# Rows of 520 columns for the normalised and the inner feed-forward activations of a two-layer encoder

## The chip, the cores and the metric

One Trainium2 chip, one core of it. The metric is the device time of one execution in microseconds. The kernel before takes 1377.04 us (median of 3 runs, 1375.52 to 1378.2).

## The reference

A two-layer encoder trunk on 512 tokens of width 1024. Layer 0 mixes by neighbourhood attention and a bidirectional state-space scan, layer 1 by grouped-query attention with rotary positions; each layer ends with a gated feed-forward part. All parts are residual. Cut to what matters here:

```python
def swiglu_ffn(x, norm_g, w13, w2):
    g, u = jnp.split(rms_norm(x, norm_g) @ w13, 2, axis=-1)   # 1024 -> 2 x 2816
    return (jax.nn.silu(g) * u) @ w2                          # 2816 -> 1024

def reference(x, ...):
    for layer in range(2):
        x = x + even_mixer(x, ...) if layer == 0 else x + odd_mixer(x, ...)
        x = x + swiglu_ffn(x, ffn_norm[layer], ffn_w13[layer], ffn_w2[layer])
    return x
```

Everything is float32.

## The kernel before, in words

All 512 tokens are held at once, features across the 128 partitions, tokens along the row: the residual stream is 8 tiles of 128 x 512. Weights are streamed from memory in blocks of 128 x 1024.

Precision comes from splitting each float32 operand into a high part that the matmul's float32r type holds, and the low rest. For the weights `load_w` (L130 to L137) does this: a DMA brings the raw block, the scalar engine writes the high part (L135), the vector engine (or GpSimd) the low one (L136). For the normalised activations `prep` (L160 to L164) does it, into two tiles made by `xgslot` (L93, L94), named xh and xl. `mm3` (L139 to L144) multiplies a split pair in three matmuls of 512 columns that accumulate in one bank: low weights by high activations (L142), high weights by low activations (L143), high by high (L144). The weight block of 128 x 128 is what a matmul loads first; the activation tile is what it streams.

`ffn` (L708 to L743) runs twice. It first splits the 8 residual tiles into 16 tiles xh and xl. Then 22 steps follow, each with one projection for the gate (banks fg) and one for the up half (banks fu), 8 triples of matmuls each; the results are scaled, gated and split again into tiles hh and hl, made by `hlane`, 44 in all. Last come 8 sums (banks fo) of 22 triples each over hh and hl, added to the residual. That is 2 x 22 x 24 = 1,056 matmuls a layer for gate and up and 8 x 66 = 528 for the second products; both layers, 2,112 and 1,056. The mixers' projections (banks g, qps, kps, q and others) stream xh and xl tiles from `xgslot` too. `oA`, layer 0's output projection, streams tiles of the mixer's pool for its first ten blocks; the last two blocks are streamed from `xgslot` tiles by `tail` (banks t), which runs right behind it. The odd layer does the same with banks o and t.

Instructions stand in the order in which this code writes them; each engine waits by semaphores for what it reads. Tiles come from pools, which are laid one behind the other along each partition, so where a tile starts follows from the sizes of the rows before it. In the built program:

| pool | what | first byte in a partition | row of one tile |
|---|---|---|---|
| `xpool`, `sp` | residual, scratch | 20,960 and 37,344 | 2,048 bytes |
| `xgpool` | 16 slots for xh, xl | 61,920 | 2,048 bytes |
| `wsp` | weight blocks, raw, high, low | 94,688 | 4,096 bytes |
| `sm` | small tiles | 127,456 | mixed, 4,320 bytes with the gap |
| `lp`, `hp0`, `op`, `hp1` in turn | mixers' tiles; hh, hl | 131,776 | 2,048 bytes for hh, hl |

From `xgpool` to `wsp` there are 32,768 bytes, a multiple of 512; a weight block of 128 columns is 512 bytes. From `wsp` to the last pools there are 37,088 bytes, 224 more than a multiple of 512.

Of the kernel before, what the change touches and what calls it, by code (L numbers as in the profile page):

```python
# [10 lines left out]
F32R = mybir.dt.float32r  # L11
# [5 lines left out]

P = 128
S = 512
D = 1024  # L20
KB = D // P
EPS = 1e-6
GRID_W = 64
ROWS = S // GRID_W
NA_H = 8
# [39 lines left out]
def encoder_kernel(ctx: ExitStack, tc: tile.TileContext, xt, vec, cst, rope, nab, w_v, w_qk, w_dt, w_ssd,  # L65
# [7 lines left out]
    xgpool = ctx.enter_context(tc.tile_pool(name="xgpool", bufs=2 * KB))  # L73
# [7 lines left out]
    def bank(name, tag="p"):  # L81
        if tag in turns:
            turns[tag].append(turns[tag].pop(0))
            tag = turns[tag][-1]
        return pp.tile([P, S], F32, name=name, tag=f"p{tag}", bufs=BANKS[tag])

    def slot(name, dt=F32):
        return sp.tile([P, S], dt, name=name, tag="s")

    def xslot(name, dt=F32):  # L90
        return xpool.tile([P, S], dt, name=name, tag="x")

    def xgslot(name):  # L93
        return xgpool.tile([P, S], F32R, name=name, tag="xg")  # L94

    def laner(pool):
        def lane(name, tag, bufs, dt=F32, cols=S):
            return pool.tile([P, cols], dt, name=name, tag=tag, bufs=bufs)
        return lane

    def small(name, cols, bufs=3, parts=P, dt=F32):
        return sm.tile([parts, cols], dt, name=name, tag=f"sm_{name}", bufs=bufs)

    def f(ap):
        return ap.bitcast(F32)
# [17 lines left out]
    def sum_rows(ps, sq, name, eng=V):  # L123
        hi, lo = slot(f"{name}_qh", F32R), slot(f"{name}_ql", F32R)
        A.activation(hi, sq, AF.Copy)
        eng.tensor_tensor(lo, sq, f(hi), ALU.subtract)
        T.matmul(ps, ones_r, lo, start=True, stop=False)
        T.matmul(ps, ones_r, hi, start=False, stop=True)

    def load_w(src, cols, name, eng=None):  # L130
        hi = wsp.tile([P, 1024], F32R, name=f"{name}_h", tag="wh", bufs=WH)
        lo = wsp.tile([P, 1024], F32R, name=f"{name}_l", tag="wl", bufs=WL)
        raw = wsp.tile([P, 1024], F32, name=f"{name}_r", tag="wr", bufs=WR)[:, 0:cols]
        nc.sync.dma_start(raw, src)
        A.activation(hi[:, 0:cols], raw, AF.Copy)  # L135
        (eng or V).tensor_tensor(lo[:, 0:cols], raw, f(hi)[:, 0:cols], ALU.subtract)  # L136
        return hi, lo  # L137

    def mm3(ps, w, wc, x, xc, first, last, wn=P):  # L139
        (wh, wl), (xh, xl) = w, x  # L140
        a, b = slice(wc, wc + wn), xc
        T.matmul(ps, wl[:, a], xh[:, b], start=first, stop=False)  # L142
        T.matmul(ps, wh[:, a], xl[:, b], start=False, stop=False)  # L143
        T.matmul(ps, wh[:, a], xh[:, b], start=False, stop=last)  # L144
# [10 lines left out]
    def project(ps, src, xg, name, eng=None):  # L155
        w = load_w(src, 1024, name, eng)
        for k in range(KB):
            mm3(ps, w, k * P, xg[k], ALL, k == 0, k == KB - 1)

    def prep(xt, g, name, mk=xgslot):  # L160
        hi, lo = mk(f"{name}_xh"), mk(f"{name}_xl")
        A.activation(hi, xt, AF.Copy, scale=g)
        V.scalar_tensor_tensor(lo, xt, g, f(hi), ALU.mult, ALU.subtract)  # L163
        return hi, lo  # L164
# [11 lines left out]
    def rsqrt_wide(ps, inv, name):  # L176
        m = slot(f"{name}_m")
        A.activation(m, ps, AF.Identity, scale=inv, bias=epst)
        return rsqrt_tile(m, name)
# [12 lines left out]
    def rsqrt_small(m, r, t):  # L192
        A.activation(r, m, AF.Ln)
        A.activation(r, r, AF.Exp, scale=-0.5)
        V.tensor_tensor(t, r, r, ALU.mult)
        V.tensor_tensor(t, t, m, ALU.mult)
        V.tensor_scalar(t, t, -0.5, 1.5, ALU.mult, ALU.add)
        V.tensor_tensor(r, r, t, ALU.mult)

    def bcast_rstd(acc, name):  # L200
        ps = bank(f"{name}_ss", "c")
        sum_rows(ps, acc, name)
        return rsqrt_wide(ps, 1.0 / D, name)

    res = [None] * KB

    def even_mixer(lp):
# [56 lines left out]
        rt, rtm, rtt = small("rt", 8, 1), small("rtm", 4, 1), small("rtt", 4, 1)  # L264
        V.tensor_scalar(rtm, pst[:, 0:4], 1.0 / D, EPS, ALU.mult, ALU.add)
        rsqrt_small(rtm, rt[:, 0:4], rtt)
# [256 lines left out]
        def ssd_group(g, gt):  # L523
# [114 lines left out]
            for i in range(2):  # L638
                yn = slot(f"yn{g}_{i}")
                V.tensor_tensor(cols(yn), pi(ys[i]), pi(r), ALU.mult)  # L640
                ssd_out[2 * g + i] = prep(yn, vc("out_norm", 2 * g + i), f"so{g}_{i}",
                                          mixslot if g < 3 else xgslot)
# [56 lines left out]
    def prep_all(gname, name):  # L699
        return [prep(res[k], vc(gname, k), f"{name}{k}") for k in range(KB)]  # L700

    def sumsq(name):
        acc = None
        for k in range(KB):
            acc = accsq(acc, res[k], name, G)
        return acc

    def ffn(layer, gname, hp):  # L708
        hlane = laner(hp)
        turns["f"] = ["p", "s", "t", "x", "s", "t", "p"]  # L710

        def fbank(name):
            return bank(name, "f")

        xg = prep_all(gname, f"f{layer}")
        hb = []
        rstd = None
        for i in range(HB):
            gp, up = fbank(f"fg{layer}_{i}"), fbank(f"fu{layer}_{i}")
            project(gp, w_fa[layer, 2 * i], xg, f"wfg{layer}_{i}")  # L720
            project(up, w_fa[layer, 2 * i + 1], xg, f"wfu{layer}_{i}")
            if i == 0:
                rstd = bcast_rstd(sumsq(f"f{layer}"), f"fr{layer}")
            g, s = slot(f"g{layer}_{i}"), slot(f"s{layer}_{i}")
            V.tensor_tensor(g, gp, rstd, ALU.mult)  # L725
            A.activation(s, g, AF.Silu)
            V.tensor_tensor(g, up, rstd, ALU.mult)  # L727
            V.tensor_tensor(g, g, s, ALU.mult)
            hi, lo = hlane(f"hh{layer}_{i}", "h", 2 * HB, F32R), hlane(f"hl{layer}_{i}", "h", 2 * HB, F32R)
            A.activation(hi, g, AF.Copy)  # L730
            V.tensor_tensor(lo, g, f(hi), ALU.subtract)
            hb.append((hi, lo))
        for o in range(KB):
            ps = fbank(f"fo{layer}_{o}")
            k0 = 0
            for j, n in enumerate(W2_SPLIT):
                w = load_w(w_fb[layer, o, :, k0 * P:(k0 + n) * P], n * P, f"wf2{layer}_{o}_{j}")
                for k in range(n):
                    mm3(ps, w, k * P, hb[k0 + k], ALL, k0 + k == 0, k0 + k == HB - 1)
                k0 += n  # L740
            V.tensor_tensor(res[o], res[o], ps, ALU.add)
            if layer == 1:
                nc.sync.dma_start(out[o], res[o])  # L743

    def odd_mixer(op):
# [51 lines left out]
        rt, rtm, rtt = small("ort", 4, 1), small("ortm", 4, 1), small("ortt", 4, 1)  # L797
        V.tensor_scalar(rtm, pst[:, 0:4], 1.0 / D, EPS, ALU.mult, ALU.add)
        rsqrt_small(rtm, rt, rtt)
        ss = bank("oss", "c")  # L800
        T.matmul(ss, ones, acc, start=True, stop=True)
        em = slot("oem")
        V.tensor_scalar(em, ss, EPS / D, EPS * EPS, ALU.mult, ALU.add)

# [206 lines left out]
    with tc.tile_pool(name="hp0", bufs=1, reuse_waits="tile") as hp:  # L1011
        ffn(0, "g_ffn0", hp)
    with tc.tile_pool(name="op", bufs=1, reuse_waits="tile") as op:
        odd_mixer(op)
    with tc.tile_pool(name="hp1", bufs=1, reuse_waits="tile") as hp:
        ffn(1, "g_ffn1", hp)
# [6 lines left out]
def _tiles(w, cols=P):  # L1023
    k, n = w.shape
    return np.ascontiguousarray(w.reshape(k // P, P, n // cols, cols).transpose(2, 1, 0, 3)).reshape(
        n // cols, P, (k // P) * cols)
# [34 lines left out]
def _layout(x):  # L1061
# [41 lines left out]
    a["w_qk"] = _tiles(w[:, 0:1024])  # L1103
    wdt = np.concatenate([w[:, 4608:4640], np.zeros((D, 32), np.float32)], 1)
    a["w_dt"] = np.ascontiguousarray(wdt.reshape(KB, P, 64).transpose(1, 0, 2)).reshape(P, KB * 64)
# [42 lines left out]
```

## Time and profile before

| | |
|---|---|
| runs | 1375.52, 1377.04, 1378.2 us |
| span of the profiled execution | 1375.2 us, first to last instruction; its own time isn't listed apart |
| matmuls (PE) | busy 1326.8 us, 96% of the span |
| weight loads (PEld) | busy 1083.7 us, 79% |
| vector engine (DVE) | busy 820.0 us, 60% |
| scalar engine (ACT) | busy 601.4 us, 44% |
| GpSimd (POOL) | busy 274.6 us, 20% |
| mean granted clock of the matmul engine | 0.988 |

The profile's rows of matmul groups read: line, engine, operation, result<-operands by the program's names, shapes, count, busy time in us, mean duration of one in ns, and the idle time of the engine just before them. A row of the timeline reads: start in us, duration in us, engine, line, operation, result<-operands, shapes, count. A matmul's duration runs past the start of the next, as they are pipelined; the distance between starts is what each one costs. The feed-forward layers stand, in us from the span's start, at about 409 to 797 (layer 0; the odd layer's first projections begin within its last 12 us) and 995 to 1371 (layer 1).

### The profile page before, as it was taken

To read this page: it belongs to the slowest core of one execution; us is meant where nothing else is said; L and a number is where in the kernel's file an instruction comes from. 1 tells how busy PE (TensorE), PEld (TensorE's weight loads), DVE (VectorE), ACT (ScalarE), POOL (GpSimd) and SP (SyncE) were. 2 spreads that over 40 slices of the span, in tenths; PEclk is the share of its full clock that TensorE was granted. 3 is DMA by queue.
4 is the path that set the end of the run, shared out by engine and by line. 5 is a ranking of instruction groups with operands and counts; after the bars stand their busy time and mean duration, and the time that the engine had idled before them with its cause. 6 is when DMAs were issued, how large, how long until landed. Compare 5 with 4: busy or idle time off the path is not lost.

```text
span 1375.2 us, 16824 instructions
## 1 busy us (share of the span) xinstructions
PE 1326.8 (96%) x6278; PEld 1083.7 (79%) x6278; DVE 820.0 (60%) x1267; ACT 601.4 (44%) x1014; POOL 274.6 (20%) x240
## 2 busy tenths in 40 slices
PE   9999898988899999999999999999999999999998
PEld 8787776766777888888888878778878888888886
DVE  6698697888847444444423377998884444443221
ACT  6674556465546323223222346777663233222210
POOL 4023344342533000000000133655230000000000
PEclk9999999999999999999999999999999999999999
DMA  7353242334442233233333344321122332333331
GB/s 229 92 154 115 87 132 95 105 98 122 124 119 90 92 100 100 93 102 97 101 95 97 97 113 94 102 60 41 47 92 92 97 102 92 98 102 92 111 110 55
DMA packets 49763, 138.83 MB, mean 101 GB/s; under 512 B 6737, under 2 KB 6865, under 8 KB 49681
## 3 DMA queue, kind: packets, MB, share of 16 engines
q1 hardware_dynamic: 49392, 137.23, 33.6%
q8 instruction: 49, 0.80, 0.2%
q10 hardware_dynamic: 288, 0.52, 0.1%
q14 instruction: 34, 0.27, 0.1%
HBM read 127.11 MB, written 2.23 MB: 94 GB/s over the span
## 4 chain that ended last, share of the span: by engine, by line
PE 67%; DVE 13%; ACT 3%; issue 2%; DMA 0%; POOL 0%; SPq 0%; DVEq 0%; ACTq 0%; POOLq 0%
PE fo L144 6%; PE fo L142 6%; PE fo L143 6%; PE fu L143 6%; PE fu L144 6%; PE fu L142 6%; PE fg L143 6%; PE fg L144 6%; PE fg L142 6%; DVE grp L493 2%; PE opt L903 1%; DVE f_xl L163 1%; PE oA L143 1%; PE oA L144 1%; PE oA L142 1%
## 5 line engine op out<-in xcount | busy, mean ns | idle before, releaser
L143 PE MATMUL fg<-f_xl,wfg_h 128*128 128x512 f32 x352 | 137.2, 390 | 3.9 <-DVE f_xl L163 3.9
L142 PE MATMUL fo<-hh,wf_l 128*128 128x512 f32 x352 | 139.2, 396 | 0.0
L143 PE MATMUL fo<-hl,wf_h 128*128 128x512 f32 x352 | 139.2, 396 | 0.0
L144 PE MATMUL fo<-hh,wf_h 128*128 128x512 f32 x352 | 139.2, 396 | 0.0
L143 PE MATMUL fu<-f_xl,wfu_h 128*128 128x512 f32 x352 | 137.7, 391 | 0.0
L144 PE MATMUL fu<-f_xh,wfu_h 128*128 128x512 f32 x352 | 137.6, 391 | 0.0
L142 PE MATMUL fu<-f_xh,wfu_l 128*128 128x512 f32 x352 | 137.5, 391 | 0.0
L144 PE MATMUL fg<-f_xh,wfg_h 128*128 128x512 f32 x352 | 136.9, 389 | 0.0
L142 PE MATMUL fg<-f_xh,wfg_l 128*128 128x512 f32 x352 | 136.9, 389 | 0.0
L136 DVE TENSOR_TENSOR wf_l<-wf_r,wf_h 128x1024 fp32r<-128x1024 f32 (+1 forms) x48 | 54.5, 1136 | 126.7 <-ACT wf_h L135 126.7
L135 ACT ACTIVATE wf_h<-wf_r 128x1024 fp32r<-128x1024 f32 (+1 forms) x48 | 47.5, 989 | 186.8 <-PE fo L144 164.4
L135 ACT ACTIVATE wfg_h<-wfg_r 128x1024 fp32r<-128x1024 f32 x44 | 46.6, 1060 | 150.8 <-issue 131.2
L727 DVE TENSOR_TENSOR g<-fu,fr_r 128x512 f32<-128x512 f32 x44 | 30.4, 691 | 124.6 <-PE fu L144 123.1
L135 ACT ACTIVATE wfu_h<-wfu_r 128x1024 fp32r<-128x1024 f32 x44 | 46.7, 1062 | 131.0 <-PE fg L144 130.4
L725 DVE TENSOR_TENSOR g<-fg,fr_r 128x512 f32<-128x512 f32 x44 | 30.2, 691 | 88.2 <-PE fg L144 88.1
L173 POOL TENSOR_TENSOR o_acc<-o_acc,o_sq 128x512 f32<-128x512 f32 x7 | 10.8, 1538 | 352.2 <-ACT o_sq L172 352.2
L143 PEld LDWEIGHTS fg<-f_xl,wfg_h 128*128 128x128 f32 x352 | 66.1, 188 | 18.5 <-DVE f_xl L163 4.8
L144 PE MATMUL g<-e_xh,w_h 128*128 128x512 f32 x192 | 79.2, 413 | 0.0
L143 PEld LDWEIGHTS fo<-hl,wf_h 128*128 128x128 f32 x352 | 66.1, 188 | 16.0
L144 PEld LDWEIGHTS fo<-hh,wf_h 128*128 128x128 f32 x352 | 66.1, 188 | 16.0
L142 PEld LDWEIGHTS fo<-hh,wf_l 128*128 128x128 f32 x352 | 66.1, 188 | 15.9
L142 PE MATMUL g<-e_xh,w_l 128*128 128x512 f32 x192 | 78.4, 408 | 0.0
(419 smaller groups left out, 3203.2 us busy)
## 6 DMA issues: line engine op xcount, KB each, us to landing
wfg_r<-in_w_fa SPq DMA_DIRECT2D x44, 512.0 KB, 3.5
wfu_r<-in_w_fa SPq DMA_DIRECT2D x44, 512.0 KB, 3.5
wf_r<-in_w_fb SPq DMA_DIRECT2D x32, 512.0 KB, 3.5
w_r<-in_w_ssd SPq DMA_DIRECT2D x24, 512.0 KB, 3.6
wf_r<-in_w_fb SPq DMA_DIRECT2D x16, 384.0 KB, 3.1
wo_r<-in_w_o SPq DMA_DIRECT2D x16, 320.0 KB, 3.0
nb<-in_nab SPq DMA_DIRECT2D x16, 256.0 KB, 3.0
ec<-ecumd SPq DMA_DIRECT2D x32, 128.0 KB, 3.1
```

Source lines behind the costliest of these rows:

```text
L135: A.activation(hi[:, 0:cols], raw, AF.Copy)
L136: (eng or V).tensor_tensor(lo[:, 0:cols], raw, f(hi)[:, 0:cols], ALU.subtract)
L142: T.matmul(ps, wl[:, a], xh[:, b], start=first, stop=False)
L143: T.matmul(ps, wh[:, a], xl[:, b], start=False, stop=False)
L144: T.matmul(ps, wh[:, a], xh[:, b], start=False, stop=last)
L163: V.scalar_tensor_tensor(lo, xt, g, f(hi), ALU.mult, ALU.subtract)
L173: eng.tensor_tensor(acc, acc, sq, ALU.add)
L493: V.scalar_tensor_tensor(o, cv[:, j:j + S], vc("conv_w", cb * 4 + j), o, ALU.mult, ALU.add)
L725: V.tensor_tensor(g, gp, rstd, ALU.mult)
L727: V.tensor_tensor(g, up, rstd, ALU.mult)
L903: T.transpose(pt[:, a * 256 + n * P:a * 256 + (n + 1) * P], pr[n][:, (2 * kp + a) * P:(2 * kp + a + 1) * P], ident)
```

## The change

The rows of the tiles that `xgslot` and, in the feed-forward part, `hlane` make become 520 columns long, and the tile that is handed out is the first 512 of them. Nothing reads or writes the other 8 columns (32 bytes). The instructions, their order on each engine and their waits are the same as before.

```diff
+SKEW = 520
...
     def xgslot(name):
-        return xgpool.tile([P, S], F32R, name=name, tag="xg")
+        return xgpool.tile([P, SKEW], F32R, name=name, tag="xg")[:, 0:S]
...
     def ffn(layer, gname, hp):
-        hlane = laner(hp)
+        def hlane(name, tag, bufs, dt):
+            return hp.tile([P, SKEW], dt, name=name, tag=tag, bufs=bufs)[:, 0:S]
+
```

So a slot of these pools is 2,080 bytes where it was 2,048, and each starts 32 bytes later, against a multiple of 2,048, than the slot before it. `xgpool` grows by 512 bytes: `wsp` now begins at 95,200 and the last pools at 132,288, where hh and hl take 91,520 bytes in place of 90,112. The rows of the mixers' own tiles keep their length.

## The prediction

> **What bounds the kernel now.** I read the page first (busy time, granted clock, chain), then a table of four stretches that lie inside the two feed-forward layers, then the groups by line, and last the order of time at places where one group of matmuls hands over to another.
>
> ```profile
> PE 1326.8 (96%) x6278; PEld 1083.7 (79%) x6278; DVE 820.0 (60%) x1267; ACT 601.4 (44%) x1014; POOL 274.6 (20%) x240
> PE 67%; DVE 13%; ACT 3%; issue 2%; DMA 0%; POOL 0%; SPq 0%; DVEq 0%; ACTq 0%; POOLq 0%
> 431.20:663.00 231.80, 231.80 (x1024) 191.99 (x1023) 109.64 (x133) 73.20 (x90) 0.00 (x0) 1.00 0.32 99
> 663.00:786.00 123.00, 123.00 (x529) 99.02 (x528) 39.03 (x42) 33.69 (x40) 8.97 (x6) 1.00 0.32 93
> 1015.30:1249.00 233.70, 233.70 (x1033) 193.53 (x1032) 110.64 (x134) 74.58 (x92) 0.00 (x0) 1.00 0.32 99
> 1249.00:1371.00 122.00, 121.94 (x523) 97.85 (x521) 30.43 (x32) 21.39 (x22) 0.00 (x0) 1.00 0.31 94
> ```
>
> The two first lines are the page's: PE is busy for 96% of the span and is 67% of the chain. The other four are the stretches (columns: length; busy time and count of PE, PEld, DVE, ACT, POOL; granted clock; DMA share; GB/s). In each PE's busy time equals the stretch or misses it by 0.06 us, and the clock is 1.00. So in the feed-forward layers no one keeps PE waiting, and the time is the number of matmuls times the distance between two starts. Nothing else can pay, and nothing else can hide a cost there.
>
> A matmul's own duration overlaps its neighbours, so I read starts. Here are two steady pieces, gate products (fg) and second products (fo); each fence shows the first row of a run and the 100th start after it.
>
> ```profile
> 499.69 0.39 PE L142 MATMUL fg<-f_xh,wfg_l 128*128 128x512 f32 x1
> ...
> 522.35 0.39 PE L143 MATMUL fg<-f_xl,wfg_h 128*128 128x512 f32 x1
> ```
>
> ```profile
> 699.75 0.40 PE L144 MATMUL fo<-hh,wf_h 128*128 128x512 f32 x1
> ...
> 723.09 0.40 PE L142 MATMUL fo<-hh,wf_l 128*128 128x512 f32 x1
> ```
>
> fg: 22.66 us for 100 starts, 226.6 ns each. fo: 23.34 us, 233.4 ns each. Shape, type and clock are the same, and so is the weight load:
>
> ```profile
> L143 PEld LDWEIGHTS fg<-f_xl,wfg_h 128*128 128x128 f32 x352 | 66.1, 188 | 18.5 <-DVE f_xl L163 4.8
> L143 PEld LDWEIGHTS fo<-hl,wf_h 128*128 128x128 f32 x352 | 66.1, 188 | 16.0
> L142 PE MATMUL fg<-f_xh,wfg_l 128*128 128x512 f32 x352 | 136.9, 389 | 0.0
> L142 PE MATMUL fo<-hh,wf_l 128*128 128x512 f32 x352 | 139.2, 396 | 0.0
> ```
>
> 188 ns on both sides; only the matmul's mean duration differs, 389 against 396 ns, by the same 7 ns as the starts. The same pair shows where layer 0's output projection (oA) gives way to its tail (t). Both multiply tiles called so, made by the same lines, but oA's lie in the mixer's pool and t's in the normalised activations' pool:
>
> ```profile
> 406.20 0.40 PE L142 MATMUL oA<-so_xh,wo_l 128*128 128x512 f32 x1
> ...
> 407.60 0.40 PE L142 MATMUL oA<-so_xh,wo_l 128*128 128x512 f32 x1
> ...
> 409.69 0.39 PE L142 MATMUL t<-so_xh,wt_l 128*128 128x512 f32 x1
> ...
> 411.05 0.39 PE L142 MATMUL t<-so_xh,wt_l 128*128 128x512 f32 x1
> ```
>
> Six starts take 1.40 us (233 ns) in oA, then 1.36 us (227 ns) in t. So the distance between starts goes with the pool that holds the moving tile. Normalised activations stand a whole multiple of 512 bytes from every weight block; tiles of the other three pools stand 224 bytes off such a multiple. I read this as the moving read and the next weight load, 188 ns long beside it, getting in each other's way more or less by their distance. Distance is exactly what the change alters.
>
> **The change part by part.** It adds and removes no instruction, and the order and the waits on every engine are as before. What the vector and scalar engines write and read keeps its 512 columns, and no DMA touches the two kinds of tile; their work, up to 110 us of a 232 us stretch in the quoted rows, is hidden by PE anyway. I cost that at nothing, and should a write to a shifted row be a few per cent dearer, PE's cover stays. The pools behind move by 512 bytes, which leaves oA (240 matmuls) and the odd mixer's o (144) at their old offset of 224. What remains is the moving read.
>
> A row of 2,080 bytes is 32.5 times 64 bytes. The two steady distances differ by 6.8 ns and are close to 34 and 35 times 6.67 ns, so the pattern repeats in some small step; I take 64 bytes for it, which is an assumption (224 is 3.5 times 64, so it fits that a half step costs). Under it a moving tile is aligned to the weights or half a step off, and every second slot of the new rows changes its kind. Counting slots in the built program: in the gate and up products (2,112 matmuls, all aligned now) 10 of 24 per projection stay aligned in layer 0 and 12 of 24 in layer 1, 44 projections each, which is 968; of the second products (1,056, all off now) one in three becomes aligned, 352. So 1,320 of 3,168 are aligned where 2,112 were: 792 more are off.
>
> Lower price, if each matmul keeps its kind's steady distance: 792 x 6.8 ns = +5.4 us (+7.8 in gate and up, -2.4 in the second products).
>
> Higher price: aligned and off now follow one another within each triple hi, lo, hi, so neither steady pattern may form. What an unsteady stretch costs shows after the wait at the start of layer 1:
>
> ```profile
> 1012.92 0.40 PE L144 MATMUL fg<-f_xh,wfg_h 128*128 128x512 f32 x1
> 1013.16 0.40 PE L142 MATMUL fu<-f_xh,wfu_l 128*128 128x512 f32 x1
> 1013.39 0.40 PE L143 MATMUL fu<-f_xl,wfu_h 128*128 128x512 f32 x1
> 1013.63 0.40 PE L144 MATMUL fu<-f_xh,wfu_h 128*128 128x512 f32 x1
> 1013.86 0.39 PE L142 MATMUL fu<-f_xh,wfu_l 128*128 128x512 f32 x1
> 1014.09 0.39 PE L143 MATMUL fu<-f_xl,wfu_h 128*128 128x512 f32 x1
> 1014.32 0.40 PE L144 MATMUL fu<-f_xh,wfu_h 128*128 128x512 f32 x1
> 1014.55 0.39 PE L142 MATMUL fu<-f_xh,wfu_l 128*128 128x512 f32 x1
> 1014.78 0.40 PE L143 MATMUL fu<-f_xl,wfu_h 128*128 128x512 f32 x1
> 1015.01 0.39 PE L144 MATMUL fu<-f_xh,wfu_h 128*128 128x512 f32 x1
> 1015.25 0.39 PE L142 MATMUL fu<-f_xh,wfu_l 128*128 128x512 f32 x1
> 1015.47 0.39 PE L143 MATMUL fu<-f_xl,wfu_h 128*128 128x512 f32 x1
> ```
>
> From 1013.16 to 1015.25 us nine starts take 2.09 us, 232.2 ns each, although every tile there is aligned; only then does the short distance set in. With all feed-forward matmuls at 232.2 ns, gate and up lose 2,112 x 5.6 = 11.8 us and the second products win 1,056 x 1.2 = 1.3: +10.5 us. I take +6.5, nearer to the lower price, because the unsteady stretch follows a stall of PE, and the changed kernel has no more of those than this one.
>
> Outside the feed-forward layers the same count gives 444 matmuls that become off: 192 of layer 0's gated projections, 80 of the odd layer's queries, 64 of layer 0's queries and keys, 64 of the tails, 44 of values and odd keys.
>
> ```profile
> L142 PE MATMUL g<-e_xh,w_l 128*128 128x512 f32 x192 | 78.4, 408 | 0.0
> L142 PE MATMUL q<-o_xh,wq_l 128*128 128x512 f32 x64 | 26.5, 414 | 0.0
> ```
>
> Their bounds are 0 and 444 x 6.8 = 3.0 us. The mean durations of 408 and 414 ns are past both steady ones: these matmuls stand among others' and seldom reach the short distance. I take +1.0.
>
> Sum: +6.5 + 1.0 = +7.5 us. The span was 1375.2 us; that execution's own time isn't listed apart, and the span is 0.3 us under the fastest run and 1.8 under the median of 1377.04. Added to the median: 1384.5 us.
>
> Here a rule of the Trainium skill speaks against me. "SBUF — State Buffer", section "Who interferes with whom", gives PE two independent read ports, one for the moving operand and one for weight loads, and says that PE never waits on anyone. By that rule the offset would not matter and the sum would be 0; this case's fg and fo, 226.6 against 233.4 ns, do not look like it, but the rows do not show the ports.
>
> **The rivals.** *Place, not distance (no change).* What splits fg from fo and t from oA may be where the tile lies in memory: normalised activations begin at byte 61,920, the other pools at 131,776 and above. The rows speak for it as much as for distance, since both change together. The pools hardly move, so 226.6 and 233.4 would stay: 1377.0. The port rule of "SBUF — State Buffer" would end there as well. Chance 0.22.
>
> *Mixed offsets agree with a short pattern (faster).* No tile now stands at several of the new offsets, and one such sequence may settle at fg's distance or below. If the second products fall to 226.6 and gate and up hold theirs, the gain is 1,056 x 6.8 = 7.2 us: 1369.8. It decides as soon as the second products gain more than gate and up lose, which is at twice the loss per matmul, since they are half as many. For it speaks that a half-step offset is the poor one in the rows and fo has nothing else; against it, that gate and up stand in the best pattern seen and can only keep it. Chance 0.20, of which 0.06 is for a deeper gain. "TensorE: Matmul & The Clock Gate", section "Back-to-back issue gap", gives 215.7 ns for this width; by that figure, an estimate from the page, all 3,168 would save about 42 us, and no run here shows such a distance.
>
> *All new offsets are poor (slower still).* If only exact multiples of 512 bytes are good, all 2,112 go to 233.4: +14.4, and +3.0 outside, 1394.4. This is the upper end of my own forecast.
>
> **How the numbers follow.** Forecast (slower) 0.58, with a range of its own of 1380 to 1394; no change 0.22; faster 0.20. The whole range must reach from the faster rival to the upper end, 1369 to 1394; past its ends lie the deeper gains and little above, under 2 in 10. About 0.2%, 2.8 us, is what a measurement of this kernel can tell from no change; the forecast's lower price of +5.4 is past that, so the chances are those of the cases.
>
> **What would show it.** Right: in the changed profile gate and up start every 229 to 232 ns in place of 226.6, the second products every 230 to 232 in place of 233.4, mean durations moving alike; oA stays at 233 and t leaves 227; PE's idle time stays as it is. A matmul count or a wait that differs would mean that something else moved. Wrong: fg's distance unchanged (place, or ports), or fo's falling by more than twice what fg's rises.

## The result, and the profile after

The changed kernel takes 1384.31 us (median of 4 runs, 1383.51 to 1385.17), the kernel before 1377.62 us (median of 4, 1375.52 to 1379.25). The ratio is 1.0055, 95% interval 1.0044 to 1.0067: slower by 6.7 us. The span of the profiled execution is 1381.7 us, 6.5 more than before.

The profile's page after: busy time and chain.

```profile
PE 1335.9 (97%) x6278; PEld 1081.7 (78%) x6278; DVE 820.8 (59%) x1267; ACT 600.9 (43%) x1014; POOL 278.2 (20%) x240
PE 67%; DVE 13%; ACT 2%; issue 2%; DMA 0%; POOL 0%; SPq 0%; DVEq 0%; ACTq 0%; POOLq 0%
```

No count has changed, DVE and ACT are busy as long as before (820.8 against 820.0, 600.9 against 601.4 us), and PE is busy 9.1 us longer. Next the groups of the feed-forward matmuls after; the lines stand one further on in the file.

```profile
L143 PE MATMUL fg<-f_xh,wfg_l 128*128 128x512 f32 x352 | 138.5, 393 | 0.0
L143 PE MATMUL fo<-hh,wf_l 128*128 128x512 f32 x352 | 138.5, 393 | 0.0
L144 PEld LDWEIGHTS fg<-f_xl,wfg_h 128*128 128x128 f32 x352 | 66.1, 188 | 19.6 <-DVE f_xl L164 4.0
L144 PEld LDWEIGHTS fo<-hl,wf_h 128*128 128x128 f32 x352 | 66.0, 188 | 15.7
```

The two kinds have come together: 393 ns on both sides, where it was 389 and 396. Weight loads are unchanged at 188 ns.

For the distance between two starts I use from here on one stretch of 200 us inside layer 1's gate and up products and one of 100 us inside its second products. The columns are: stretch; length; PE's busy time and count; granted clock; DMA share; GB/s. A matmul lasts about 0.39 us, so 1.7 of those counted began ahead of the stretch: the distance is the length divided by the count less 1.7. A count is whole, and one matmul more or less is 0.3 ns in a stretch of 200 us and 0.5 ns in one of 100 us; smaller differences can't be told apart. Before:

```profile
1020.00:1220.00 200.00, 200.00 (x884) 1.00 0.31 96
1262.00:1362.00 100.00, 100.00 (x430) 1.00 0.35 105
```

After:

```profile
440.00:640.00 200.00, 200.00 (x867) 1.00 0.31 95
1020.00:1220.00 200.00, 200.00 (x861) 1.00 0.31 95
1262.00:1362.00 100.00, 100.00 (x434) 1.00 0.36 107
```

Before: 200 / 882.3 = 226.7 ns and 100 / 428.3 = 233.5. After: gate and up 231.1 in layer 0 (the first row) and 232.7 in layer 1, second products 231.3. PE fills every stretch, so this is the whole change inside them: 1,056 x 4.4 + 1,056 x 6.0 - 1,056 x 2.2 ns is +8.7 us, good to about half a microsecond.

The place where oA gives way to the tail t, after:

```profile
408.05 0.40 PE L144 MATMUL oA<-so_xl,wo_h 128*128 128x512 f32 x1
408.28 0.40 PE L145 MATMUL oA<-so_xh,wo_h 128*128 128x512 f32 x1
408.51 0.40 PE L143 MATMUL t<-so_xh,wt_l 128*128 128x512 f32 x1
408.75 0.40 PE L144 MATMUL t<-so_xl,wt_h 128*128 128x512 f32 x1
408.98 0.40 PE L145 MATMUL t<-so_xh,wt_h 128*128 128x512 f32 x1
409.21 0.39 PE L143 MATMUL t<-so_xh,wt_l 128*128 128x512 f32 x1
...
410.61 0.40 PE L143 MATMUL t<-so_xh,wt_l 128*128 128x512 f32 x1
```

There is no step any more: six starts in t take 1.40 us, as they did in oA before. The durations change between 0.39 and 0.40 us, where t settled at 0.39 after its first few matmuls before.

Of the 8.7 us the span shows 6.5. Taken from start to start, the gate and up products with their one wait go from 243.68 to 246.66 us in layer 0 and from 242.09 to 248.09 in layer 1, the second products from 122.97 to 121.85 and 121.83: +6.7 in all. What is missing against 8.7 is mainly in layer 0, in this pair of rows, before and then after, just behind the wait for the first low tiles:

```profile
426.40:430.00 3.60, 3.60 (x10) 2.88 (x11) 3.20 (x3) 1.69 (x2) 1.02 (x1) 0.60 0.44 134
```

```profile
426.60:430.00 3.40, 3.40 (x15) 2.78 (x16) 3.06 (x3) 1.70 (x2) 1.02 (x1) 1.00 0.45 136
```

Before, the granted clock falls to a mean of 0.60 there, and 10 matmuls are counted in 3.60 us; after, 15 in 3.40 at full clock. So the kernel before loses some 1.4 us here (3.60 x 0.40) that the changed one does not. The wait itself is shorter too after the change, by 0.4 us in each layer: 1.56 us where it was 1.97 and 1.94. A half-clock stretch stands once more in the odd layer of the kernel before:

```profile
920.00:932.00 12.00, 9.53 (x49) 0.86 0.37 93
```

```profile
920.00:932.00 12.00, 9.54 (x57) 1.00 0.25 69
```

First before, then after; 12.00 x 0.14 is 1.7 us, and less where PE waits anyway. The two stretches favour the changed kernel by at most some 3 us in this pair of profiles. The other executions of these two kernels have no trace, so whether it holds there is not shown.

### The profile page after: what moved, and what is told of

It reads as the page before. It is cut to its first block, busy times and chain, and to the rows that moved or that the text cites. A ratio compares the mean times of both kernels' runs of the same rounds, so it can differ in the third digit from the quotient of the medians.

```text
span 1381.7 us, 16824 instructions
## 1 busy us (share of the span) xinstructions
PE 1335.9 (97%) x6278; PEld 1081.7 (78%) x6278; DVE 820.8 (59%) x1267; ACT 600.9 (43%) x1014; POOL 278.2 (20%) x240
## 4 chain that ended last, share of the span: by engine, by line
PE 67%; DVE 13%; ACT 2%; issue 2%; DMA 0%; POOL 0%; SPq 0%; DVEq 0%; ACTq 0%; POOLq 0%
PE fu L144 6%; PE fo L145 6%; PE fu L145 6%; PE fu L143 6%; PE fo L143 6%; PE fo L144 6%; PE fg L144 6%; PE fg L145 6%; PE fg L143 6%; DVE grp L494 2%; PE opt L906 1%; DVE f_xl L164 1%; PE oA L144 1%; PE oA L145 1%; PE oA L143 1%
## 5 line engine op out<-in xcount | busy, mean ns | idle before, releaser
L143 PEld LDWEIGHTS fg<-f_xh,wfg_l 128*128 128x128 f32 x352 | 66.2, 188 | 15.7
L143 PEld LDWEIGHTS fu<-f_xh,wfu_l 128*128 128x128 f32 x352 | 66.2, 188 | 15.7
```

## The experiments

The theory to test: the distance in bytes from a moving tile's start to the weight blocks, or rather its remainder by some step such as 64 or 256, sets the time between matmul starts. The rivals: the tile's place in memory as such; the mixing, that is, any change of offset from one matmul to the next; and the shift of the pools behind. "Offset" below is the moving tile's start less that of the weight block, in bytes. All kernels start from the kernel before.

**One half of the change alone.** `xg_rows_only` and `h_rows_only`:

```diff
-        return xgpool.tile([P, S], F32R, name=name, tag="xg")
+        return xgpool.tile([P, 520], F32R, name=name, tag="xg")[:, 0:0+S]
```

```diff
-        hlane = laner(hp)
+        def hlane(name, tag, bufs, dt):
+            return hp.tile([P, 520], dt, name=name, tag=tag, bufs=bufs)[:, 0:0+S]
```

> Only the normalised activations get rows of 520; hh and hl keep 512. Distance theory (the start of a moving tile against the weight blocks, by 64 bytes, sets the distance between matmul starts): gate and up as in the changed kernel, 231.3 ns in layer 0 and 232.8 in layer 1; second products stay at 233.3. Time about 9 us over the kernel before, 1386.6. Growth theory (what costs is that the pools behind moved by 512 bytes, not the rows): as in the changed kernel, 1384.3, with the second products at 231.2.

> Only hh and hl get rows of 520. Distance theory: gate and up stay at 226.7 ns, second products start every 231.2 ns in place of 233.3, 1.1 us less in each layer: 1375.3, faster than before by 2.3 us. Mixing theory (any change of offset from matmul to matmul costs, whatever the values): second products no shorter than 233.3, time 1377.6 or above.

Measured: 1386.72 us with the normalised tiles alone (ratio 1.0070, 1.0052 to 1.0087), 1373.89 us with hh and hl alone (0.9979, 0.9969 to 0.9989), each against 1377.06 (median of 21 runs). The sum of the two, +9.7 and -3.2, is +6.5, the whole change within the noise. Stretches of the first, then of the second kernel:

```profile
1020.00:1220.00 200.00, 200.00 (x861) 1.00 0.31 97
1262.00:1362.00 100.00, 100.00 (x431) 1.00 0.37 110
```

```profile
1020.00:1220.00 200.00, 200.00 (x884) 1.00 0.32 98
1262.00:1362.00 100.00, 100.00 (x434) 1.00 0.33 103
```

Each half moves its own matmuls and leaves the others: 232.7 and 232.9 ns, then 226.7 and 231.3. The shift of the pools behind does nothing: in the first kernel they move by 512 bytes, and the second products stay. The mixing theory in its plain form (any change costs, whatever the values) falls with the second kernel, since mixed offsets are better there than the even one of 224.

**A gap in front of the last pools**, `gap_288`: rows as before, but a small tile is 288 bytes larger, so that every pool stands a multiple of 512 from the weights.

```diff
-        zt = small("zt", P, 1)
+        zt = small("zt", P + 72, 1)[:, 0:P]
```

> Rows as before, but one small tile is 288 bytes larger, so that all pools behind it start a whole multiple of 512 bytes from the weight blocks. Distance theory: second products, oA and o go from 233.3 to 226.7 ns between starts; 1,056 + 240 + 144 matmuls at 6.7 ns is 9.6 us, of which I expect 9: 1368.6. Place theory (tiles above byte 131,776 are slow as such): 233.3 stays, 1377.6.

Measured: 1367.10 us, ratio 0.9923 (0.9905 to 0.9941): 10.0 us faster than the kernel before, and so faster than both. Its stretches (the second one earlier, as it ends sooner) and groups:

```profile
1020.00:1220.00 200.00, 200.00 (x884) 1.00 0.31 97
1250.00:1350.00 100.00, 100.00 (x443) 1.00 0.37 109
```

```profile
L144 PE MATMUL fg<-f_xh,wfg_h 128*128 128x512 f32 x352 | 136.9, 389 | 0.0
L142 PE MATMUL fo<-hh,wf_l 128*128 128x512 f32 x352 | 136.9, 389 | 0.0
```

The second products start every 100 / 441.3 = 226.6 ns, where they had 233.5, and last 389 ns like the gate's. The tiles stand 288 bytes higher than before and are fast, so place as such is out.

**Rows of 528 columns**, `rows_528`: 528 in place of 520 in both pools, so that offsets change by multiples of 64 bytes, the step that the prediction assumed.

> Both kinds of tile get rows of 528 columns, 2,112 bytes, 33 times 64: the offset to the weights changes from matmul to matmul by multiples of 64 bytes only. Distance theory with a step of 64 bytes: gate and up 226.7 ns, second products 233.3, time as before, 1377.6. If only whole multiples of 512 are good, or if any change from matmul to matmul costs (mixing theory): gate and up at 231 ns or above, time 1384 or above.

Measured: 1384.62 us, ratio 1.0052 (1.0039 to 1.0065).

```profile
1020.00:1220.00 200.00, 200.00 (x869) 1.00 0.31 97
1262.00:1362.00 100.00, 100.00 (x431) 1.00 0.35 107
```

Gate and up at 230.6 ns, not 226.7. Either 64 bytes is not the step, or the change from matmul to matmul costs. That called for even offsets, the same for each matmul of a group.

**Even offsets.** A pad ahead of the weight blocks (of p bytes) sets the normalised tiles' offset to -p; a larger small tile sets that of the last pools. For -32 and 0:

```diff
     wsp = ctx.enter_context(tc.tile_pool(name="wsp", bufs=1))
+    wsp.tile([P, 8], F32, name="wpad", tag="wpad", bufs=1)
...
-        zt = small("zt", P, 1)
+        zt = small("zt", P + 72, 1)[:, 0:P]
```

The others have 16 and 8, 32 and 48, 56 and 24, 40 and 40 in place of 8 and 72.

> Rows as before, but the weight blocks stand 32 bytes further on (normalised activations at offset -32 for every matmul) and the last pools at offset 0. Step theory (a value's remainder by a small step decides; 32 is half a step): gate and up 233.3 ns for every matmul, second products 226.7. Mixing theory (only a change of offset from matmul to matmul costs; any even offset settles at its own steady distance): no value given beforehand, but one steady pattern. Time about 1385 with the first.

> Rows as before; every normalised tile at offset -64, every tile of the last pools at offset 256. If 64 bytes is the step and rows of 528 columns were slow through mixing alone: 226.7 ns in gate, up and second products, 1367. If offset -64 is poor as such: gate and up at 230 ns or above, with 256 telling the same for its half of 512.

> Rows as before; every normalised tile at offset -128, every tile of the last pools at -96. Step of 64: 226.7 ns in gate and up, 233.3 in the second products, 1377. Step of 128: the same for gate and up, and second products at some other steady value. Only multiples of 512 (or 256) good: gate and up at 230 ns or above.

> Rows as before; every normalised tile at offset 288 (32 past 256), every tile of the last pools at 320 (64 past 256). Step theory with 256 bytes: both poor, 230 to 235 ns, as at the other four offsets measured that are no multiple of 256; time 1385 or above. A gain below 226.7 would be new.

> Rows as before; every normalised tile at offset 352 (96 past 256), every tile of the last pools at 384 (128 past 256). Step theory with 256 bytes: second products 232.4 ns, as gate and up had at 384; gate and up 230 to 235. Time 1383 or above.

One run each, so what follows rests on the distances and not on the times; the kernel before took 1377.88 us beside the first three and 1375.21 beside the last two. Times, in the order above: 1380.08, 1381.12, 1383.26, 1383.35 and 1387.98. The second products' rows, in the same order, one fence for each kernel:

```profile
1262.00:1362.00 100.00, 100.00 (x443) 1.00 0.36 109
```

```profile
1262.00:1362.00 100.00, 100.00 (x443) 1.00 0.36 108
```

```profile
1262.00:1362.00 100.00, 100.00 (x428) 1.00 0.35 107
```

```profile
1262.00:1362.00 100.00, 100.00 (x438) 1.00 0.35 107
```

```profile
1262.00:1362.00 100.00, 100.00 (x430) 1.00 0.37 112
```

And the rows of gate and up for the first and the third; those of the second, fourth and fifth show x859 as well:

```profile
1020.00:1220.00 200.00, 200.00 (x859) 1.00 0.31 94
```

```profile
1020.00:1220.00 200.00, 200.00 (x862) 1.00 0.31 95
```

Put together by the remainder of the offset by 256, as means over a stretch:

| remainder | distance between starts, ns | from offset |
|---|---|---|
| 0 | 226.7, 226.6, 226.6 | 0 in gate and up (before); 0 and 256 in the second products |
| 32 | 233.3 | 288, gate and up |
| 64 | 229.2 | 320, second products |
| 96 | 233.3 | 352, gate and up |
| 128 | 232.5 and 233.5 | -128, gate and up; 384, second products |
| 160 | 234.6 | -96, second products |
| 192 | 233.3 | -64, gate and up |
| 224 | 233.3 and 233.5 | -32, gate and up; 224, second products (before) |

Of the remainders tried, in steps of 32 bytes, only 0 is good, 64 lies between, and all else is 6 to 8 ns dearer. At remainder 0 each start in these stretches comes 225 to 228 ns after the last one; elsewhere the single distances mostly vary, at -128 between 228 and 241. At -64 they are steady: all 858 in the stretch are 233 or 234 ns, while DVE is busy for 93 and ACT for 63 us of the 200. A clash with what these two write now and then would show in some matmuls and not in all, so at this offset it is not that.

Two of the expectations failed at offset 320: 230 to 235 ns and 1385 us or above were expected, 229.2 and 1383.35 measured.

In the kernel with -32 only the weight blocks have moved against the normalised tiles, which stand where they stood, and still all 2,112 matmuls over them slow down: it is the distance between the two that counts. Its time was foretold at about 1385, a forecast that has the 7 us that its second products gain in it already; it came to 1380.08. Between the two profiles, gate and up take 5.0 us more in layer 0 and 6.5 in layer 1, where 1,056 x 6.6 ns is 7.0, since the kernel before has the longer waits and, in layer 0, the half-clock stretch; and everything outside the feed-forward layers takes 1.4 us less.

**Mixed offsets, both ways.** `lows_64` and `lows_256` are the kernel with the gap of 288 bytes, with the low tiles in a pool region of their own that begins 64 or 256 bytes further on, so that each triple streams offsets 0, 64, 0 or 0, 256, 0 (16 columns below for 64 bytes, 64 columns for 256):

```diff
-        hlane = laner(hp)
+        def hlane(name, tag, bufs, dt):
+            if name[:2] == "hl" and not hb:
+                hp.tile([P, 16], F32, name=f"hgap{layer}", tag="gap", bufs=1)
+            return hp.tile([P, S], dt, name=name, tag="l" if name[1] == "l" else "h", bufs=HB)
```

> As the kernel with the gap of 288 bytes, but the low tiles hl stand 64 bytes further on: second products stream offsets 0, 64, 0 in each triple; all else at 0. Mixing theory: second products above 229 ns although both offsets would be good alone. Step theory with 64: 226.7, time as with the gap of 288 bytes, 1367. If 64 is poor as such: between 227 and 234.

> As the kernel with the gap of 288 bytes, but the low tiles hl stand 256 bytes further on: second products stream offsets 0, 256, 0 in each triple. Step theory with 256 bytes: 226.7 ns, time as with the gap, 1367. Mixing theory (a change from matmul to matmul costs by itself): 230 ns or above, 1370 to 1376.

Measured: 1375.58 us with 64 (1377.88 before), 1368.94 with 256 (1375.21 before). Second products, 64 and then 256:

```profile
1262.00:1362.00 100.00, 100.00 (x433) 1.00 0.34 105
```

```profile
1250.00:1350.00 100.00, 100.00 (x443) 1.00 0.36 109
```

231.9 ns against 226.6. A change of offset by 256 is free. A change by 64 costs more than its parts: even runs of 0 and of 64 take 226.7 and 229.2, so two to one would be 227.5. So in this sequence the mixing costs by itself, 4.4 ns, since the remainder by 256 changes.

That is not a rule for all sequences. With rows of 528 columns, layer 1's gate and up matmuls stand at remainders 0, 64, 128 and 192 in equal parts (slots counted in the built program, as for the prediction). The table's mean over these is (226.7 + 229.2 + 232.5 + 233.3) / 4 = 230.4 ns, and 230.6 was measured. In the changed kernel all eight remainders occur. Weighted by their counts, the table gives 232.2 ns for gate and up in layer 0, 232.0 in layer 1 and 232.6 for the second products; measured were 231.1, 232.7 and 231.3. So most of the changed kernel's loss needs no cost of mixing: few of its gate and up matmuls are left at a good remainder. The order of the offsets then shifts the distance by about 1 ns, one way or the other; what decides which way is not shown.

**All of it 32 bytes on**, `all_32_on`: the kernel with the gap, and 32 bytes more in the first pool of all.

```diff
-    vect = kp.tile([P, NVEC], F32, name="vect")
+    vect = kp.tile([P, NVEC + 8], F32, name="vect")[:, 0:NVEC]
```

> As the kernel with the gap of 288 bytes, but everything, normalised activations, weight blocks and last pools, stands 32 bytes further on; all offsets stay 0. Distance theory: 226.7 ns everywhere, 1367. Place theory in a small form (a tile's own start by 256 bytes counts, whatever the weights'): gate, up and second products at 232 to 234 ns, 1385 or above.

Measured: 1369.60 us (1375.21 before), both stretches at 226.7 ns:

```profile
1020.00:1220.00 200.00, 200.00 (x884) 1.00 0.30 96
1250.00:1350.00 100.00, 100.00 (x443) 1.00 0.35 107
```

A tile's own start does not matter here, only that against the weights. This rests on the two stretches; the time is of a single run, and its 5.6 us less than the kernel before are fewer than the 10.0 of the gap alone.

## Why the prediction was right, and where it was not

*What bounds the feed-forward layers.* Right in the main: PE has no idle time in any stretch, before or after, and the change of time inside them is a change of the distance between starts. That nothing else could hide a cost was too strong. The stretches begin behind each layer's one wait, and that wait and the half clock behind it hid some 2 us of the loss.

*Distance, not place.* Right, and shown: moving the weights alone by 32 bytes slows gate and up, moving everything by 32 bytes leaves all at 226.7 ns, and the second products become fast at a higher address.

*The step of 64 bytes.* Wrong: it is 256. With it goes the count of 1,320 aligned matmuls: by 256 the same slots give 360 of the 3,168, 264 in gate and up and 96 in the second products. The two multiples of 6.67 ns from which I had read the step give no such size, and the reading that 224 is half a step off was a coincidence; 224 is simply no multiple of 256.

*The two prices.* In gate and up the higher one's number held: 4.4 and 6.0 ns against the 5.6 of the unsteady stretch, about 11.0 us against 11.8 (the lower price said 7.8). In the second products the lower one's gain was nearer: 2.3 us against 2.4 and 1.3. Together +8.7 where I took +6.5, so this term was too small. The higher price's mechanism, that alternation by itself costs, is not what the table shows. Its even distances by the right step, weighted by the remainders, give +11.4 in gate and up and -1.0 in the second products. So the lower price's method, each matmul at its own kind's distance, would have asked about +10.4 with the step of 256, and that the unsteady stretch's 5.6 ns came so near is luck as far as the runs tell. My reason for staying near the lower price, that an unsteady stretch follows a stall, did not hold either: in the changed kernel the distances vary between 225 and 237 ns throughout layer 1's stretch, with no stall in it. Layer 1's 232.7 also lies above the 229 to 232 that I had named as the sign of being right.

*The terms outside.* I took +1.0. Between the two profiles the stretches differ by +0.6 us in the gated projections, where other engines keep PE waiting, -0.4 around oA, +0.3 in each of the two tails and some -1.0 in the odd layer, where the half-clock stretch of the kernel before is worth up to 1.7. Together that is -0.2, so no loss shows outside, though the half clock may hide up to 1.7. That the median came within 0.2 us of the forecast is partly luck: a feed-forward term 2.2 too small, an outer term 1.0 too large, and in the kernel before the longer waits and the two half-clock stretches, which the changed kernel's profile lacks.

*The ports.* By the rule of the Trainium skill ("SBUF — State Buffer", section "Who interferes with whom") that PE's two read ports are independent and PE waits on no one, the gap of 288 bytes would be without effect. It gained 10.0 us; the measurement decides. What lies beneath, which of the two reads is held up and by what, no run here shows, and whether the block in use or the one being loaded counts was not tried.

*The rivals.* Place is out. The faster rival had a true core: mixed remainders are better for the second products than 224, by 2.2 ns; but gate and up, twice as many, had the best remainder to lose. The slower rival was nearer to the mechanism than my own count: seven of eight gate and up matmuls do stand at a poorer remainder now, only that not all of these cost 6.8 ns. No run came below 226.6 ns, so the deeper gain has no support. The 215.7 ns given for it stand on the page of the Trainium skill that is named there ("TensorE: Matmul & The Clock Gate"), but in its section "Wait — 56ns, not 53.3ns?".

## What to carry to other kernels

When matmuls run back to back, compare the distance between starts of groups with the same shape: a few ns that go with the tile's pool and not with its maker point to addresses. Here, with float32r weight blocks of 128 x 128 and 512 columns streamed, a moving tile should start a whole multiple of 256 bytes from the weight blocks; pools with odd-sized small tiles between them break that, and 288 bytes of padding bring it back for 10.0 us. Spreading tiles over offsets is no safe default: it takes the best offset away along with the bad ones. And a steady stretch tells what one matmul costs, not what the span will lose: add the waits and the granted clock around it.

## What the runs showed of the hardware that was not expected

- Matmul streams of the same kind run at different mean distances by the offset alone, 226.7 to 234.6 ns. At multiples of 256 bytes each start comes 225 to 228 ns after the last one; at the others the single distances mostly vary, within 224 to 241.
- A wait of PE of 1.97 us ahead of one matmul was followed by a stretch at about half clock in the kernel before (mean 0.60 over 3.6 us); the wait of 1.56 us at the same place in the changed kernel was not. Each of the fourteen kernels' profiles has this wait twice, once in each feed-forward layer. Twelve of them last 1.93 to 2.00 us, in the kernels whose gate and up products start every 226.7 ns; behind eight of these the clock falls to half for some 3.4 us. Sixteen last 1.46 to 1.70 us, in the kernels with slower gate and up products, and behind none of these does it fall. So part of what the faster distance gains can be lost again at this wait; why the clock stays full behind four of the twelve is not shown.

The two waits, before and then after:

```profile
426.33 0.50 PE L143 MATMUL fg<-f_xl,wfg_h 128*128 128x512 f32 x1 [1.97 <-DVE f_xl L163]
```

```profile
426.54 0.50 PE L144 MATMUL fg<-f_xl,wfg_h 128*128 128x512 f32 x1 [1.56 <-DVE f_xl L164]
```
